# A two-layer decoder trunk on one core: plain fp32 products for three chunks of the first projection and half an out-projection, x loaded first, gate rows through DRAM, and a new order of steps

## The chip, the cores and the metric

One core of a Trainium2 chip. The metric is device time of one execution in microseconds (us), lower is better. The kernel before takes 633.34 us (median of 3 runs, 632.42 to 634.86).

## The reference

256 tokens of width 1024 go through two layers. Each layer has an attention sub-layer and an MLP; each of them is modulated by a conditioning vector c and closed by a LayerNorm:

```
mod = silu(c) @ ada_w + ada_b                    # per layer: shift1, scale1, gate1, shift2, scale2, gate2
h = x * (1 + scale1) + shift1
y = attention(h)                                 # h @ w_in -> q, k, v; rope; causal softmax; @ w_out
x = layer_norm(ALPHA * x + (1 + gate1) * y)      # layer 0: 16 heads of 64; layer 1: differential attention
h = x * (1 + scale2) + shift2
y = square(relu(h @ w_up)) @ w_down              # 1024 -> 4096 -> 1024
x = layer_norm(ALPHA * x + (1 + gate2) * y)
```

All data is float32. With one block of 256 keys, the block selection of layer 0 chooses nothing, and it is plain causal attention.

## The kernel before

The tokens are two blocks b of 128. Each dense product is made of 128x128 by 128x512 pieces, and keeps fp32 accuracy by **splitting**: both operands are written as hi + lo in the rounded type fp32r, and hi·hi, hi·lo and lo·hi are added in PSUM (`mm3`, `dense`, `dense2`: three matmuls for one product). A weight arrives by DMA in a raw tile (three buffers of 1 MB); `split_piece` makes hi with a cast on ACT (L499) and lo with a subtraction on DVE (L500), 1024 columns at a time, into eight buffers each. The activations are split in the same way.

The six vectors of `mod` are computed on DVE (`ada_rows`, L571 to L579): 128 rows of the transposed ada_w (512 KB, a tile aw) are multiplied by silu(c), spread over all partitions in sbc, and summed along the row. There are 96 such pieces. For the columns aw has two buffers; the first scale rows use the three buffers of bc.

**The first projection** is written out ahead of the table of steps. `first_operand(j)` takes chunk j of eight (128 of the 1024 input features): two pieces of ada, a slice of x, 768 KB of w_in (half of v, and q and k of head groups 0 and 1), a transposition of x on PE (L925), the modulation on ACT (L927), the split of both. `first_products(j)` adds 18 matmuls to six PSUM banks `kacc`. The other columns come later in `load_cols`: v group 1 (step v01), q and k of groups 2 and 3.

**The order** of everything else comes from the table `PROGRAM`: one word is one step. `aLVJ` is ada piece J of vector V in layer L, `V` and `Q` are projections (layer, block, group), `T` transposes q and k, `S` and `P` are scores and values of one (block, group), `o` and `O` load and multiply w_out, `G` spreads a gate vector over the partitions, `N` prepares the modulation after a LayerNorm, `C` is residual, LayerNorm and modulation of a block, `u`, `U`, `X`, `Y`, `d`, `D` are the MLP. `plan_issue` then simulates the engines with a table of costs and fixes each engine's queue: of what is ready it takes the instruction that stands first in the table. All loads go through SP's one queue, which issues in order and stands still while a load waits for its buffer.

The gate vector lies in columns (feature on partition). `step_gate` calls `bcast_cols`: eight PE transpositions of a column spread to 128x128 (L483) and two copies from PSUM on ACT (L485).

In layer 0 the attention has a score matmul of 64 rows for each head (L799), transposed probabilities (L780) and value matmuls (L873); these and layer 1's L839 are fp32 matmuls without a split, and each leaves two records in the trace. `split_oT` splits the attention's output, `out_proj` multiplies it. After the MLP of layer 1 comes a tail (`close_last`).

Of the kernel before, what the change touches and what calls it, by code (L numbers as in the profile page):

```python
# [21 lines left out]
P = 128  # L22
D = 1024
# [27 lines left out]
    u04 Y04 a051 a052 a116 a107 D002 a133 a140 d03 a120 u07 a130 Y06 a102 a142 a145 D011 d04 u05 D003 a144 a106
    D004 a105 Y05 a143 a146 D012 D013 D014 a057 Y07 a104 d05 D005 d06 D006 a115 D015 d07 D007 a111 G01 a114 a117
    N01 a135 C001 D016 D017 C011 v10 V100 q10 Q100 Q110 a136 a151 q11 V110 T100 Q111 T110 K01 S11 a123 Q101 a124
    R011 q12 T111 S10 a156 q13 Q103 Q113 T101 S12 P10 T103 a134 Q102 a132 S13 v11 o10 a125 Q112 a122 o11 u11 u10
    u14 a131 S16 F10 T102 P12 S14 F12 T112 V111 P11 d10 P13 a154 V101 P14 a155 F11 d11 P16 a126 a127 T113 u12
# [69 lines left out]
def _cost(i, e, psum_names):  # L125
# [4 lines left out]
    if e == 4:  # L130
# [3 lines left out]
        if "float32r" in str(aps[0].dtype):  # L134
            return (227 if n > 256 else 117 if n > 128 else 109), 170 + n * 0.43
# [42 lines left out]
class Planner:  # L178
# [3 lines left out]
    def __init__(self, ins, slots, psum_names, groups):  # L182
# [11 lines left out]
        for k, i in enumerate(ins):  # L194
# [9 lines left out]
            def hits(t, pm, fm, j, p2, f2):  # L204
                return p2 & pm and f2 & fm or t in psum_names and eng[j] != eng[k]
# [221 lines left out]
def tile_trunk(ctx: ExitStack, tc: tile.TileContext, x, c, moba_w_in, moba_w_out, diff_w_in, diff_w_out,  # L427
# [765 lines left out]
```

## Time and profile before

| | |
|---|---|
| median of 3 runs | 633.34 us |
| profiled execution | 632.71 us, of it 630.5 us between the first and the last instruction |
| PE, busy | 603.7 us (96%) |
| DVE, busy | 501.2 us (79%) |
| ACT, busy | 383.0 us (61%) |
| DMA | 158.25 MB, 251 GB/s over the span |

A PE record is longer than the time from one matmul's start to the next (a 128x512 matmul is shown with some 400 ns), so records overlap, a PE that is shown busy can still be slowed, and the pace of a run of matmuls is what counts. The other 2.2 us of the execution lie before the first and after the last instruction.

### The profile page before, as it was taken

What the parts mean: (1) busy time and instruction counts of PE and PEld (TensorE: products, weight loads), DVE (VectorE), ACT (ScalarE), POOL (GpSimd) and SP (SyncE); (2) the same over time, 40 slices, a digit from 0 to 9 for tenths busy, and PEclk for the clock granted to TensorE, in tenths of its full rate; (3) what the DMA queues carried; (4) which work ended last, traced back from release to release, by engine and by line L of the source; (5) the groups of instructions that cost most, each with busy time, mean ns of one, the idle gap of its engine ahead of it and who ended that gap; (6) DMA issues with size and microseconds to landing.
All of it is one profiled execution on the core that took longest, in us unless ns stands there. A gap on an engine that the chain in (4) does not pass through costs nothing.

```text
span 630.5 us, 8816 instructions
## 1 busy us (share of the span) xinstructions
PE 603.7 (96%) x3148; PEld 493.3 (78%) x3148; DVE 501.2 (79%) x899; ACT 383.0 (61%) x711; POOL 21.7 (3%) x36
## 2 busy tenths in 40 slices
PE   4999999989999999999999999999999999999995
PEld 3776776767788888888877878887788888888884
DVE  4899989899998887988799999868767556464557
ACT  3457788867745755565386566767657576363730
POOL 0000000011000000000011000111000000000001
PEclk9999999998999999999999999999999999999998
DMA  8999969878898987989777977333646664646201
GB/s 289 407 337 397 360 241 328 302 244 305 299 394 326 304 325 249 350 328 333 247 260 270 333 239 254 122 122 120 213 139 211 236 216 140 232 161 225 110 0 68
DMA packets 66086, 158.25 MB, mean 251 GB/s; under 512 B 4057, under 2 KB 21370, under 8 KB 66042
## 3 DMA queue, kind: packets, MB, share of 16 engines
q1 hardware_dynamic: 66042, 157.68, 70.3%
q8 instruction: 25, 0.41, 0.3%
q14 instruction: 19, 0.16, 0.1%
HBM read 156.62 MB, written 1.05 MB: 250 GB/s over the span
## 4 chain that ended last, share of the span: by engine, by line
PE 83%; DMA 7%; DVE 6%; issue 1%; POOL 1%; ACT 1%; SPq 1%; DVEq 0%; ACTq 0%; POOLq 0%
PE ac L553 18%; PE sc L553 12%; PE mm L1091 7%; PE tp L1091 7%; PE mm L536 7%; PE mm L538 7%; PE mm L537 7%; PE mm L1096 4%; PE tp L1096 4%; DMA raw<-in_moba_w_in_dram 3%; DMA aw<-in_ada_w_dram 2%; PE sc L799 2%; DVE lo L500 1%; PE tp L780 1%; PE tp L749 1%
## 5 line engine op out<-in xcount | busy, mean ns | idle before, releaser
L500 DVE TENSOR_TENSOR lo<-raw,hi 128x1024 fp32r<-128x1024 f32 x196 | 231.3, 1197 | 54.6 <-ACT hi L499 51.5
L499 ACT CAST hi<-raw 128x1024 fp32r<-128x1024 f32 x196 | 200.5, 1034 | 101.5 <-PE sc L553 41.0
L578 DVE CUSTOM_DVE_ANT_0 aw<-aw,sbc,tabT 128x1024 f32<-128x1024 f32 x96 | 121.6, 1278 | 8.9 <-DMA aw<-in_ada_w_dram 8.5
L536 PE MATMUL mm<-hi,hT 128*128 128x512 f32 x224 | 91.6, 410 | 6.8 <-ACT hT L676 3.3
L537 PE MATMUL mm<-lo,hT 128*128 128x512 f32 x224 | 89.5, 402 | 1.8 <-DVE lo L500 1.8
L538 PE MATMUL mm<-hi,hT 128*128 128x512 f32 x224 | 88.9, 399 | 0.3
L1091 PE MATMUL mm<-hT,hi 128*128 128x512 f32 x192 | 61.2, 396 | 0.0
L1091 PE MATMUL tp<-hT,hi 128*128 128x512 f32 x192 | 60.6, 395 | 0.0
L536 PEld LDWEIGHTS mm<-hi,hT 128*128 128x128 f32 x224 | 42.8, 191 | 17.2 <-ACT hT L676 4.2
L553 PE MATMUL ac<-lo,sTh 128*128 128x512 f32 x160 | 51.7, 397 | 0.0
L553 PE MATMUL ac<-hi,sTh 128*128 128x512 f32 x160 | 51.3, 396 | 0.0
L537 PEld LDWEIGHTS mm<-lo,hT 128*128 128x128 f32 x224 | 42.6, 190 | 11.2 <-DVE lo L500 3.0
L538 PEld LDWEIGHTS mm<-hi,hT 128*128 128x128 f32 x224 | 42.5, 190 | 10.7 <-DVE hT L677 2.1
L553 PE MATMUL ac<-hi,sTl 128*128 128x512 f32 x160 | 50.2, 392 | 0.0
L553 PE MATMUL sc<-lo,sTh 128*128 128x512 f32 x144 | 45.9, 394 | 0.0
L553 PE MATMUL sc<-hi,sTl 128*128 128x512 f32 x144 | 45.5, 393 | 0.0
L553 PE MATMUL sc<-hi,sTh 128*128 128x512 f32 x144 | 45.4, 393 | 0.0
L1096 PEld LDWEIGHTS tp<-hT,lo 128*128 128x128 f32 x192 | 34.7, 188 | 7.6
L1096 PEld LDWEIGHTS mm<-hT,lo 128*128 128x128 f32 x192 | 34.4, 188 | 7.1 <-DVE lo L500 0.2
L1096 PE MATMUL mm<-hT,lo 128*128 128x256 f32 x192 | 36.9, 279 | 0.0
L1096 PE MATMUL tp<-hT,lo 128*128 128x256 f32 x192 | 36.6, 279 | 0.0
L553 PEld LDWEIGHTS ac<-hi,sTh 128*128 128x128 f32 x160 | 29.5, 188 | 6.9 <-ACT hi L499 0.6
(173 smaller groups left out, 874.1 us busy)
## 6 DMA issues: line engine op xcount, KB each, us to landing
aw<-in_ada_w_dram SPq DMA_DIRECT2D x96, 512.0 KB, 5.4
raw<-in_mlp_w_up_dram SPq DMA_DIRECT2D x32, 1024.0 KB, 6.0
raw<-in_mlp_w_down_dram SPq DMA_DIRECT2D x32, 1024.0 KB, 7.0
raw<-in_diff_w_in_dram SPq DMA_DIRECT2D x16, 512.0 KB, 4.6
raw<-in_moba_w_in_dram SPq DMA_DIRECT2D x24, 256.0 KB, 6.9
raw<-in_moba_w_in_dram SPq DMA_DIRECT2D x8, 512.0 KB, 5.2
raw<-in_moba_w_out_dram SPq DMA_DIRECT2D x4, 1024.0 KB, 5.6
raw<-in_diff_w_in_dram SPq DMA_DIRECT2D x4, 1024.0 KB, 5.1
```

The lines of the kernel that those rows point to most:

```text
L499: act.copy(out=hi[:, :n], in_=raw_ap)
L500: vec.tensor_tensor(out=lo[:, :n], in0=raw_ap, in1=hi[:, :n], op=ALU.subtract)
L536: pe.matmul(dst, lhsT=xh, rhs=wh, start=start, stop=False)
L537: pe.matmul(dst, lhsT=xh, rhs=wl, start=False, stop=False)
L538: pe.matmul(dst, lhsT=xl, rhs=wh, start=False, stop=stop)
L553: pe.matmul(dsts[h], lhsT=a, rhs=w[:, h * 512:(h + 1) * 512], start=start and k == 0 and i == 0, stop=stop and k == n - 1 and i == 2)
L578: vec.tensor_tensor_reduce(out=aw, in0=aw, in1=sbc, scale=1.0, scalar=adab_cols(l, v)[:, j:j + 1], op0=ALU.mult, op1=ALU.add, accum_out=dst)
L749: pe.transpose(out=tp[:, i * P:(i + 1) * P], in_=nat[:, i * P:(i + 1) * P], identity=ident)
L780: pe.transpose(out=tp[:, s_ * P:(s_ + 1) * P], in_=mats[m][:, kb * P:(kb + 1) * P], identity=ident)
L799: pe.matmul(r[i, cpt][:, kb * P:(kb + 1) * P], lhsT=qk[l, b, g][rows, i, :], rhs=qk[l, kb, g][rows, 2 + i, :], start=True, stop=True)
L1091: pe.matmul(ps, lhsT=w[k][0][:, c_], rhs=x3[k], start=first, stop=last)
L1096: pe.matmul(ps[:, 0:S], lhsT=w[k][1][:, c_], rhs=x3[k][:, 0:S], start=False, stop=False)
```

## The change

- **Plain products in the first projection.** Chunks 0, 1 and 2 are not split: PE multiplies fp32 x by fp32 raw weights straight from the raw tile (24 matmuls in place of 72). Chunks 3 to 7 stay split. All 1024 columns of v are taken, so a chunk is 1 MB and eight products, and `kacc` takes all eight PSUM banks; step v01 with its 48 matmuls is gone from the later part.
- **x first.** Both blocks of x are loaded whole, the first ahead of all ada rows, transposed four chunks at a time, and kept in xT; the modulation then works in place.
- **Unread transposes.** 30 transpositions of sbc (`step_warm`) are put on PE among those of x. Nothing reads them.
- **Half the out-projection plain.** Feature half 1 of layer 0's w_out is loaded into hi and lo buffers as it is and multiplied in fp32 (`PLAINO` is (1,); 16 matmuls in place of 48); its oT isn't split.
- **Gate rows through DRAM.** A gate is one 128x8 transposition, a small copy on ACT, a write of 4 KB to DRAM and a broadcast load of 512 KB.
- **Two DVE operations of the rope become one**, and every second ada piece of layer 0's gate1, shift2 and scale2 uses bc's three buffers.
- **New order**: the first projection's steps are in the table now, and the whole table is another one (in the planner two numbers and one rule on PSUM change with it).

```diff
 PROGRAM = """
-    Q000 a020 V000 a046 v01 V010 Q001 a100 a043 V011 a024 a036 T000 S00 a032 Q010 a023 a045 q02 P00 a040 a025
+    W6 I1 A0 W5 I0 M0 B0 A1 M1 B1 m1 A2 B2 A3 A4 M4 A5 A6 W4 J0 B3 J1 B4 M2 A7 M7 m2 M6 B5 B6 M3 M5 J2 B7 a100
...
+    def plain_rows(w, r0):
+        ts = plain_tiles()
+        for k, t in enumerate(ts):
+            sp.dma_start(out=t, in_=w[r0 + k * P:r0 + (k + 1) * P, :])
+        return ts
...
-        ada_rows(l, v, j, cl[:, j:j + 1], "aw", 2)
+        tag = ("bc", 3) if l == 0 and v in (GATE1, SHIFT2, SCALE2) and j % 2 else ("aw", 2)
+        ada_rows(l, v, j, cl[:, j:j + 1], *tag)
...
+    PLAIN0 = (0, 1, 2,)
+    def step_warm(st, n):
+        ps = psum("ac")
+        for k in range(2 * n):
+            pe.transpose(out=ps[:, (k % 4) * P:(k % 4 + 1) * P], in_=sbc[:, (k % 8) * P:(k % 8 + 1) * P], identity=ident)
...
+        for s_ in (0, 2, 3, 1):
+            for b in range(2):
+                if j in PLAIN0:
+                    pe.matmul(kacc[b][(0, 3, 1, 2)[s_]], lhsT=xT[j // 4][:, j % 4, b * P:(b + 1) * P], rhs=ws[s_],
+                              start=j == 0, stop=j == KC - 1)
+                    continue
+                hi, lo = halves(hT0[j // 4], b)
+                mm3(kacc[b][(0, 3, 1, 2)[s_]], (hi[:, j % 4, :], lo[:, j % 4, :]), ws[s_], j == 0, j == KC - 1)
...
+        if l == 0 and g2 in PLAINO:
+            for k in range(4):
+                for h in range(2):
+                    pe.matmul(dsts[h], lhsT=oT[l, g2][:, k, b * P:(b + 1) * P], rhs=rows[k][:, h * 512:(h + 1) * 512],
+                              start=g2 == 0 and k == 0, stop=g2 == 1 and k == 3)
+            return
...
+    def step_gate_row(st, l, i):
+        row = st["row", l, i] = dram.tile([KC, P], F32, tag="row", name="row", bufs=1)
+        rs = small.tile([KC, P], F32, tag="grow", name="grow", bufs=1)
+        tp = psum("tp")
+        pe.transpose(out=tp[0:KC, 0:P], in_=cols[l, GATE1 if i == 0 else GATE2], identity=ident)
+        act.copy(out=rs, in_=tp[0:KC, 0:P])
+        sp.dma_start(out=row, in_=rs)
     def step_gate(st, l, i):
         g = st["gate", l, i] = ap_.tile([P, D], F32, tag="bc", name="gate", bufs=3)
-        bcast_cols(g, cols[l, GATE1 if i == 0 else GATE2])
+        row = st.pop(("row", l, i))
+        sp.dma_start(out=g, in_=row.rearrange("k p -> (k p)")[None, :].to_broadcast([P, D]))
```

Where the instructions stand. **PE, from its first instruction**, before (sbc and ccol: silu(c) and its columns; t: the table of biases; cs: the identity):

```order
L483 MATMUL tp<-cs,ccol 128x128 x8
L944 MATMUL tp<-cs,t_73 128x128
L925 MATMUL tp<-cs,x 128x128 x4
L536 MATMUL mm<-hi,hT 128x512
L536 MATMUL sc<-hi,hT 128x512
L536 MATMUL ac<-hi,hT 128x512
```

and now:

```order
L487 MATMUL tp<-cs,ccol 128x128 x8
L932 MATMUL tp<-cs,t_75 128x128
L954 MATMUL ac<-cs,sbc 128x128 x18
L942 MATMUL tp<-cs,x 128x128 x8
L954 MATMUL ac<-cs,sbc 128x128 x12
L942 MATMUL tp<-cs,x 128x128 x8
L995 MATMUL mm<-raw,xT 128x512 x2
L995 MATMUL sc<-raw,xT 128x512 x2
```

The unread transposes (L954) stand in PE's queue ahead of those of x, and all 16 transposes of x now stand ahead of the first product.

**DVE, from the mean and variance of the first LayerNorm (layer 0, block 0)**, before (col_530 and col_600 are scale2 and shift2; A and B, the modulation that ACT waits for; lo is the split of the MLP's weights):

```order
L652 BN_AGGR bna<-bns 128x2
L500 TENSOR_TENSOR lo<-raw,hi 128x1024
L578 ISA aw,col_530<-aw,sbc,tabT 128x1024
...
L594 TENSOR_TENSOR A_1411<-col_530,tabT 128x8
L595 TENSOR_TENSOR B_1412<-col_530,tabT_100 128x8
L500 TENSOR_TENSOR lo<-raw,hi 128x1024
L578 ISA aw,col_600<-aw,sbc,tabT 128x1024
L578 ISA col_600 128x1
L500 TENSOR_TENSOR lo<-raw,hi 128x1024
L596 TENSOR_TENSOR B_1412<-B_1412,col_600 128x8
```

and now (col_538 and col_555):

```order
L618 TENSOR_TENSOR A_1337<-col_538,tabT 128x8
L619 TENSOR_TENSOR B_1338<-col_538,tabT_102 128x8
L675 BN_STATS bns<-z 128x6
L503 TENSOR_TENSOR lo<-raw,hi 128x1024
L601 ISA aw,col_555<-aw,sbc,tabT 128x1024
L601 ISA col_555 128x1
L676 BN_AGGR bna<-bns 128x2
L620 TENSOR_TENSOR B_1338<-B_1338,col_555 128x8
```

A and B were finished after three ada pieces and four splits that stood behind the statistics; now B comes directly behind them, with the last ada piece ahead.

**SP, the loads around layer 0's first gate**, now (row and gate are the new write and broadcast load; the first LayerNorm needs gate, the modulation needs the three aw behind it):

```order
L600 DMA aw<-in_ada_w_dram 128x1024 x3
L1048 DMA row<-grow 8x128
L600 DMA aw<-in_ada_w_dram 128x1024 x2
L1053 DMA gate<-row 128x1024
L600 DMA aw<-in_ada_w_dram 128x1024 x3
L646 DMA bc<-in_ln_g_dram 128x1024
```

The gate's load stands two pieces of ada behind the write that it reads, and 41.8 MB of loads stand ahead of it in the queue, by the shapes; the last of the three aw ends at 43.4 MB. Before, the last ada piece of this LayerNorm ended at 43.9 MB.

## Rows read from the trace of the kernel before

**Rows 1.** The page's busy times by engine: us (share of the span), instructions.

```profile
PE 603.7 (96%) x3148; PEld 493.3 (78%) x3148; DVE 501.2 (79%) x899; ACT 383.0 (61%) x711; POOL 21.7 (3%) x36
```

**Rows 2.** Busy time of each engine between the LayerNorms (the cuts are the starts of BN_AGGR: layer 0 attention b0 130.8, b1 146.4, its MLP 318.5 and 331.5, layer 1 attention 430.7 and 447.9, its MLP 615.2). Columns: stretch, length, busy us and instructions of PE, PEld, DVE, ACT, POOL, then granted clock, DMA share, GB/s.

```profile
0.00:130.80 130.80, 116.43 (x659) 89.86 (x660) 112.88 (x267) 88.79 (x205) 0.29 (x5) 1.00 0.89 329
130.80:146.40 15.60, 12.37 (x52) 9.43 (x52) 15.14 (x29) 11.45 (x18) 2.54 (x2) 0.89 0.84 291
146.40:318.50 172.10, 172.10 (x861) 144.18 (x860) 149.21 (x202) 98.11 (x144) 2.56 (x2) 1.00 0.87 313
331.50:430.70 99.20, 99.00 (x555) 79.80 (x555) 88.02 (x232) 65.73 (x169) 9.36 (x18) 1.00 0.62 213
430.70:447.90 17.20, 16.64 (x76) 12.50 (x75) 15.98 (x22) 12.33 (x20) 1.25 (x3) 1.00 0.72 240
447.90:615.20 167.30, 167.16 (x840) 140.49 (x839) 96.32 (x115) 96.42 (x141) 0.81 (x2) 1.00 0.47 164
```

**Rows 3.** The same view with cuts at the start, the end of the first projection (52.4), the end of layer 0's out-projection (139.4), and the MLP's first products.

```profile
3.50:12.00 8.50, 3.33 (x13) 2.47 (x13) 3.43 (x8) 3.30 (x7) 0.00 (x0) 1.00 1.00 346
12.00:16.00 4.00, 3.97 (x9) 3.18 (x10) 3.99 (x5) 1.00 (x2) 0.00 (x0) 1.00 1.05 394
16.00:20.00 4.00, 4.00 (x21) 3.30 (x20) 3.73 (x8) 1.92 (x5) 0.00 (x0) 1.00 1.02 406
12.00:52.40 40.40, 37.73 (x156) 29.13 (x157) 37.46 (x78) 20.47 (x42) 0.00 (x0) 1.00 0.99 377
52.40:139.40 87.00, 83.81 (x532) 64.98 (x531) 79.59 (x195) 69.17 (x161) 2.54 (x2) 1.00 0.85 304
139.40:142.90 3.50, 0.44 (x3) 0.01 (x2) 3.50 (x7) 2.42 (x7) 0.00 (x0) 0.92 1.04 407
142.90:146.40 3.50, 3.50 (x10) 2.69 (x11) 3.50 (x7) 3.40 (x6) 0.00 (x0) 0.59 1.04 378
```

**Rows 4.** Undisturbed runs of one kind of matmul on the chain that ended last: start us, length us, engine, output, line, records.

```profile
124.30 1.05 PE mm L873 x16
357.28 1.09 PE sc L799 x16
428.12 0.97 PE mm L839 x8
514.89 0.87 PE tp L483 x8
600.63 10.89 PE ac L553 x48
```

**Rows 5.** The start, instructions in order of time: start us, length us, engine, line, operation, out<-in, shapes, count, and the idle time before with what ended it.

```profile
3.53 1.94 PE L483 MATMUL tp<-cs,ccol 128*128 128x128 f32 x8 [3.53 <-DMA cs<-in_constants_dram]
8.40 1.09 PE L925 MATMUL tp<-cs,x 128*128 128x128 f32 x4 [2.63 <-DMA x<-in_x_dram]
10.93 1.56 ACT L499 CAST hi<-raw 128x1024 fp32r<-128x1024 f32 x2 [0.53 <-DMA raw<-in_moba_w_in_dram]
12.03 0.80 PE L536 MATMUL mm<-hi,hT 128*128 128x512 f32 x1 [2.55 <-ACT hi L499]
```

**Rows 6.** PE's waits on the split and on the attention's chain, the same view.

```profile
25.86 0.50 PE L537 MATMUL mm<-lo,hT 128*128 128x512 f32 x1 [0.48 <-DVE lo L500]
39.25 0.44 PE L925 MATMUL tp<-cs,x 128*128 128x128 f32 x2 [1.26 <-ACT full L927]
55.42 0.50 PE L537 MATMUL mm<-lo,hT 128*128 128x512 f32 x1 [1.15 <-DVE lo L500]
110.46 0.66 PE L780 MATMUL tp<-cs,p 128*128 128x128 f32 x4 [0.53 <-ACT pT L782]
```

**Rows 7.** Groups of DVE and ACT instructions of the whole span: line, engine, operation, out<-in, shapes, count | busy us, mean ns of one | idle before, with its causes.

```profile
L500 DVE TENSOR_TENSOR lo<-raw,hi 128x1024 fp32r<-128x1024 f32 x188 | 226.3, 1219 | 54.6 <-ACT hi L499 51.5
L500 DVE TENSOR_TENSOR lo<-raw,hi 128x512 fp32r<-128x512 f32 x8 | 5.5, 682 | 0.0
L931 DVE TENSOR_TENSOR hT<-full,hT 128x128 fp32r<-128x128 f32 x16 | 3.9, 284 | 2.2 <-ACT hT L930 2.2
L892 DVE TENSOR_TENSOR sTl<-ac,sTh 128x256 fp32r<-128x256 f32 x4 | 1.7, 420 | 0.9 <-ACT sTh L891 0.9
L499 ACT CAST hi<-raw 128x1024 fp32r<-128x1024 f32 x188 | 196.2, 1052 | 101.5 <-PE sc L553 41.0 <-PE tp L1091 22.4 <-DMA raw<-in_moba_w_in_dram 14.0
```

**Rows 8.** Around the first LayerNorm of layer 0, instructions in order of time (SPq is SP's queue; the length of a load there is the time that it holds the queue).

```profile
124.56 9.05 SPq L577 DMA_DIRECT2D aw<-in_ada_w_dram  x3
139.15 1.22 DVE L500 TENSOR_TENSOR lo<-raw,hi 128x1024 fp32r<-128x1024 f32 x1
140.29 0.16 DVE L596 TENSOR_TENSOR B<-B,col 128x8 f32<-128x8 f32 x1
140.48 1.85 ACT L673 ACTIVATE full<-tp,B,A 128x128 f32<-128x128 f32 x5 [2.30 <-DVE B L596]
142.89 0.80 PE L536 MATMUL mm<-hi,hT 128*128 128x512 f32 x1 [3.06 <-ACT hT L676]
```

**Rows 9.** What SP's queue waited for, 60 to 150 us: us in total, times, longest.

```profile
SPq L577 <- DVE col L578: 21.2, 12, 3.2
```

**Rows 10.** Loads: out<-in, engine, operation, count, KB each, median us from issue to landing.

```profile
bc<-in_ln_g_dram SPq DMA_DIRECT2D x4, 512.0 KB, 7.3
ccol<-in_c_dram SPq DMA_DIRECT2D x1, 4.0 KB, 1.6
```

More of the change, by code (lines that the diff above doesn't have):

```diff
@@ L51 @@
[L51 to L55, printed above, removed]
@@ L402, in run @@
         return r
-    store = type(s_.bass_ap.tensor).__name__ == "Tile"
+    t = s_.bass_ap.tensor
+    store = type(t).__name__ == "Tile" and str(t.space) != "DRAM"
     on, off = (s_, o) if store else (o, s_)
@@ L885, in split_oT @@
         key = l, g // 2
+        if l == 0 and g // 2 in PLAINO:
+            if key not in oT:
+                oT[key] = ap_.tile([P, 4, 2 * P], F32, tag="sTh", name="oT", bufs=2)
+            act.copy(out=oT[key][:, (g % 2) * 2:(g % 2) * 2 + 2, b * P:(b + 1) * P],
+                     in_=tp[:, 0:256].rearrange("p (k t) -> p k t", t=P))
+            return
         if key not in oT:
@@ L967, in tile_trunk @@
-    vec.reduce_sum(out=ldot, in_=lprod, axis=AX.X)
-    act.activation(out=ldot, in_=ldot, func=AF.Exp)
-    vec.tensor_tensor(out=ldot[:, 0:1], in0=ldot[:, 1:2], in1=ldot[:, 0:1], op=ALU.subtract)
-    vec.tensor_scalar(out=ldot[:, 0:1], in0=ldot[:, 0:1], scalar1=-LAMBDA_INIT, scalar2=None, op0=ALU.add)
-    nlam = small.tile([P, 1], F32, name="nlam")
-    tps = psum("tp")
-    pe.matmul(tps[:, 0:1], lhsT=ones[0:1, :], rhs=ldot[:, 0:1], start=True, stop=True)
-    vec.tensor_copy(out=nlam, in_=tps[:, 0:1])
+    xT = [ap_.tile([P, 4, 2 * P], F32, tag="sTl", name="xT", bufs=2) for _ in range(2)]
@@ new lines, in step_first_weights @@
+    def step_first_weights(st, j):
+        raw = raw_tile()
+        wr = moba_w_in[0][j * P:(j + 1) * P, :]
+        sp.dma_start(out=raw[:, 0:1024], in_=wr[:, 2 * D:3 * D])
+        for s_ in range(2):
+            sp.dma_start(out=raw[:, 1024:2048].rearrange("p (g s n) -> p s g n", g=2, s=2)[:, s_],
+                         in_=wr[:, s_ * D:s_ * D + 512].rearrange("p (g n) -> p g n", n=256))
+        if j in PLAIN0:
+            st["w0", j] = [raw[:, i * 512:(i + 1) * 512] for i in range(4)]
+            return
+        st["w0", j] = [(h_[:, c_:c_ + 512], l_[:, c_:c_ + 512])
+                       for h_, l_ in (split_piece(raw[:, 0:1024]), split_piece(raw[:, 1024:2048])) for c_ in (0, 512)]
@@ L1030, in step_v @@
     def step_v(st, l, b, g2):
-        if l == 0 and g2 == 0:
-            ps = kacc[b][0]
+        if l == 0:
+            ps = kacc[b][3 * g2]
         else:
@@ L1042, in step_qk @@
             w = st["wq", l, g]
-            ps = unit(w, block_ops(st["x", 2 * l], b))
+            if l == 0 and g in PLAIN:
+                ps = psum("mm")
+                for k in range(KC):
+                    pe.matmul(ps, lhsT=xT[k // 4][:, k % 4, b * P:(b + 1) * P], rhs=w[k], start=k == 0, stop=k == KC - 1)
+            else:
+                ps = unit(w, block_ops(st["x", 2 * l], b))
         rope_qk(l, b, g, ps)
```

173 lines of the change are left out of this document (99 added, 74 removed).

## The prediction

> **What bounds the kernel now.** I read the busy times first, then the busy time between the LayerNorms, then the pace of undisturbed matmuls, and last PE's waits in the stretches where it lost time. The page says PE is busy 96% of the span [rows 1]: only less work on PE, or less waiting in the few places that still wait, can shorten it. In the two MLPs PE is busy all the time (172.1 of 172.1 us, 167.2 of 167.3) [rows 2]; there nothing is to be won but PE work. Layer 0's attention is another matter: to the second LayerNorm at 146.4 us DVE is busy 112.9 + 15.1 = 128.0 us [rows 2], 91% of the time since it began at about 6 us, and DMA's share is 0.89 over the first 130.8 us. Three engines are close to their limits there, and they stop each other.
>
> How much PE loses there follows from paces. A 128x512 fp32r matmul takes 10.89 / 48 = 0.227 us, a transposition 0.87 / 8 = 0.109, and 16 records of layer 0's scores or values take 1.09 and 1.05 us [rows 4]. The first projection is 144 matmuls and 12 transposes of x between 12.0 and 52.4 us (156 records) [rows 3]: 32.7 + 1.3 = 34.0 us of work in 40.4. From there to the end of the out-projection at 139.4 stand 48 matmuls for v group 1, 96 for q and k, 96 for the out-projection (54.5 us), 96 transposes (10.5), and 96 records each of scores and values (12.8): 77.8 us of work in 87.0. So PE loses 6.4 + 9.2 = 15.6 us between 12.0 and 139.4. Behind that it stands 3.5 us until the MLP's first product, which waits for B, late on DVE [rows 8], and then the granted clock is 0.59 for 3.5 us [rows 3]: eight products at the lower level, 1.2 GHz, some 0.2 us longer each, 1.6 us. Compared with a PE that never stopped, the MLP begins at 139.4 + 3.5 + 1.6 = 144.5.
>
> **The change, part by part.**
>
> *Plain products.* 40 fp32 matmuls take the place of 120. The trace has no plain 512-column product, but it has full fp32 products of 128 columns: 8 records, four products, in 0.97 us, the last record's end included [rows 4]. By columns that is at most 0.97 us for 512 columns; four passes at the price of the fp32r matmul are 0.91. A group of eight ends with a tail that a row of products doesn't show, so I take 0.89 and keep 0.85 to 0.97. Each costs 0.89 - 0.68 = 0.21 us more on PE than the three that it replaces, 8.4 us in all. What goes is off PE: up to the second LayerNorm DVE loses eight splits of 512 columns (8 x 0.682 = 5.5), four net of 1024 (4.9), four of oT (1.7) and two or so of hT and the rope [rows 7], 14.3 us together, so 113.7 us are left. ACT loses about as much, which ends nothing, since it waits itself.
>
> *The start.* Ahead of the first weights 2.2 MB are loaded in both orders; they were there at 10.9 us [rows 5], x now with them. Four transposes, a copy and a modulation on ACT then take about 1.6 us, the first half of the weights comes 0.52 MB later (1.5 us at 346 GB/s [rows 3]), and no split follows. First product at 13.0 instead of 12.03. All transposes of x are then done. In the four us from 12.0 PE got through 9 matmuls, in the next four 21 [rows 3]: the pace of 1.2 GHz, although the row prints a clock of 1.00. That cost 2.0 us. The 30 unread transposes fill the time from 5.5 us; I take it that after them the first products run at the full pace.
>
> *What the sum takes for the attention.* Work on PE from the first product: 24 x 0.89 + 120 x 0.227 = 48.6 us for the first projection with all of v, then 96 x 0.227 = 21.8, out-projection 48 x 0.227 + 16 x 0.89 = 25.1, 89 transposes 9.7, scores and values 12.8: 118.0 us. That ends at 131.0 plus the waits. Of the 15.6 us of waits now, 2.0 are the low clock, 4.4 the split and ada in the first projection and 1.2 lo of v group 1 [rows 6]; the plain chunks and the empty v01 step take most of these away. About 8 are the attention's chains between PE, DVE and ACT. DVE's share falls from 91% to 113.7 of about 137 us, 83%, and q and k products of two groups now stand between the attention's pieces. I keep 7 us of waits; the bounds are 1 and the 15.6 of now. The MLP then begins at 138.0 without the gap: B stands directly behind the statistics, and PE has out-projection work of block 1 (12.6 us) while block 0 is normalized. Gain 144.5 - 138.0 = **6.5 us**.
>
> *DMA.* The last ada piece that this LayerNorm needs ends at 43.4 MB in SP's queue; at 377 GB/s [rows 3] that is 118 us, ahead of the 130 or so at which it is wanted. What held the queue were ada buffers (SP waited 21.2 us for DVE's col in 60 to 150 us [rows 9], 9.05 us for one group of three [rows 8]); there are five of them now for these vectors. Cost 0, with this cover of some 10 us.
>
> *Gates.* Seven PE transposes fewer each. The one in the attention is counted above; the other three give 21 x 0.109 = **2.3 us** in stretches where PE is always busy. The load is queued tens of products ahead in the MLPs, so the way through DRAM costs nothing there.
>
> *Layer 1.* Same work, another order; DVE keeps its 104 us of 116 between 331.5 and 447.9 [rows 2]. 0, with 4 us to either side.
>
> *Sum.* 630.5 - 6.5 - 2.3 = 621.7 us of span; with the 2.2 us around it, **624 us**. The profiled execution (632.71) is 0.6 below the median of the runs, which doesn't move the forecast. A measurement of this kernel can tell about 0.5%, 3.2 us, from no change: 630.2 to 636.5 counts as the same.
>
> **The rivals.**
>
> *The clock stays low at the start.* Thirteen transposes ran before 12.03 us and the first products still went at 0.43 us [rows 3, 5]; but PE had been idle for 2.55 us before them, so the trace leaves it open. If transposes don't raise the clock, those in the queue take 0.217 each (1.94 us for eight with the tail [rows 5]), the second x comes through 2.5 us later and the first 4 us lose 2.0 again: 624 + 4.5 = 628.5. The Trainium skill (TensorE: Matmul & The Clock Gate, Part 4: PE-mode transpose) says just this, that transposes don't count as busy for the clock. By that rule the unread transposes are a loss, and the sum is 628.5. Chance 0.18.
>
> *The waits stay.* Each of the three engines has less to do or the same, but chains of latency decide, not shares: 15.6 us of waits instead of 7 give 632.6. For it: PE waited for ACT and DVE in pieces of half a us [rows 6], which a freer DVE need not shorten. Against it: the new order puts more independent products between them. Chance 0.17.
>
> *The waits all but vanish*, and layer 1 gains too: 1.5 us instead of 7, and 4 us from layer 1, 614.5. Chance 0.12.
>
> *The gate comes late.* The gate no longer costs 1.5 us on PE and ACT but a write that must land (1.6 us for a small transfer), a wait of SP's queue for it and a load of 512 KB (7.3 us for such a broadcast) [rows 10]: 7.4 us more on LayerNorm's chain. At the same time a raw buffer of a plain chunk is freed only after its products (7.1 us for 2.1 MB, 295 GB/s instead of 377), which over three chunks costs DMA 4.7 us. If the loads are what block 0's LayerNorm waits for, the MLP begins 12.1 us later and the kernel takes 630.5 + 12.1 - 2.3 + 2.2 = 642.5, slower. It decides from the point where the gate's load is issued less than about 10 us before block 0's out-projection ends. Against it: 10 us of cover by the DMA sum above. Chance 0.08.
>
> **How the numbers follow.** The forecast (618 to 630) has 0.45, the rivals 0.18, 0.17, 0.12 and 0.08. Faster: nearly all of the forecast, the last but one, two thirds of the low clock and a little of the case of the waits, 0.72. Same: most of the case of the waits and the rest of the low clock, 0.18. Slower: the late gate and a bad order of layer 1 on top of the waits, 0.10. The range 614.5 to 636 leaves out the late gate and half of the best case; the bounds of the plain product (40 x 0.04 below, 40 x 0.08 above) lie inside.
>
> **What would show it.** Plain products at about 0.45 us a record and two records each; the first at 13 us and at that pace at once (right) or at 0.86 (low clock); 48 to 50 us of first projection with waits under 3 us; the MLP's first product about 138 us with no gap and a granted clock of 1.00 ahead of it; DVE near 114 us to the second LayerNorm; two short records of SP around the gate. The prediction is wrong if the plain product costs over 1 us, if PE waits for gate or B in layer 0, or if layer 1's attention takes over 120 us.

## The result: 624.4 us, 1.4% less time

The changed kernel takes 624.4 us (median of 4 runs, 623.45 to 624.98); the kernel before took 633.20 beside it (median of 4). The ratio is 0.9856, with an interval of 0.9833 to 0.9880. The profiled execution has a span of 622.4 us, 8.1 less than before. The forecast was 624.0.

The page's busy times, to be held against [rows 1]: PE works 1.6 us more in a span that is 8.1 us shorter, DVE and ACT some 13 to 17 us less.

```profile
PE 605.3 (97%) x3110; PEld 485.4 (78%) x3110; DVE 484.6 (78%) x857; ACT 370.3 (59%) x689; POOL 27.2 (4%) x36
```

The changed kernel's busy time between the LayerNorms, columns as in [rows 2]:

```profile
0.00:129.10 129.10, 123.67 (x662) 89.04 (x663) 104.76 (x243) 82.67 (x190) 0.29 (x5) 1.00 0.96 353
129.10:141.50 12.40, 11.25 (x42) 6.74 (x40) 11.43 (x20) 6.97 (x14) 2.60 (x2) 1.00 0.64 214
141.50:311.60 170.10, 169.59 (x845) 142.01 (x844) 143.88 (x196) 96.79 (x143) 2.48 (x2) 1.00 0.86 309
324.40:426.70 102.30, 101.03 (x563) 81.03 (x562) 91.70 (x232) 68.92 (x172) 11.87 (x18) 1.00 0.65 222
426.70:439.50 12.80, 12.16 (x58) 9.58 (x57) 11.32 (x18) 9.73 (x17) 2.49 (x2) 1.00 0.63 205
439.50:607.10 167.60, 167.45 (x835) 139.86 (x834) 97.96 (x116) 94.97 (x139) 2.49 (x2) 1.00 0.52 176
```

In the first stretch DMA's share rose from 0.89 to 0.96. The granted clock, 0.89 between layer 0's two LayerNorms before, is 1.00. In layer 1 the attention became longer and the stretch between its LayerNorms shorter, 115.1 us together after 116.4; its MLP is as long as before (167.6 and 167.3).

PE from 5 to 18 us, in order of time (start, length, count, and the idle time before with what ended it):

```profile
5.38 3.79 PE L954 MATMUL ac<-cs,sbc 128*128 128x128 f32 x18
9.00 1.04 PE L942 MATMUL tp<-cs,x 128*128 128x128 f32 x8
9.88 1.47 PE L954 MATMUL ac<-cs,sbc 128*128 128x128 f32 x12
12.21 1.06 PE L942 MATMUL tp<-cs,x 128*128 128x128 f32 x8 [0.86 <-DMA x<-in_x_dram]
14.49 1.98 PE L995 MATMUL mm<-raw,xT 128*128 128x512 f32 x4 [1.22 <-ACT xT L978]
16.31 1.88 PE L995 MATMUL sc<-raw,xT 128*128 128x512 f32 x4
```

Eighteen unread transposes take 3.79 us, the eight of x behind them 1.04. The granted clock is printed as 1.00 for this whole stretch, so the pace has to tell: up to about 8.8 us the transposes start 0.213 us apart, behind it 0.109, which is the step from the lower level (1.2 GHz) to the higher (2.4 GHz), behind nothing but transposes. The second half of x came late, and the first plain product starts at 14.49. From its second record on the plain products run at 0.429 us per record, two records each: 0.859 us.

PE's stretches up to the MLP (columns as in [rows 2]; at 135.50 the last record of the out-projection begins, at 137.25 the MLP's first product):

```profile
14.49:60.00 45.51, 45.51 (x158) 29.62 (x159) 36.71 (x61) 20.02 (x30) 0.00 (x0) 1.00 1.04 401
60.00:135.50 75.50, 75.50 (x471) 54.25 (x470) 69.98 (x184) 59.17 (x154) 2.60 (x2) 1.00 0.92 329
135.50:137.25 1.75, 0.60 (x2) 0.00 (x0) 1.75 (x3) 1.75 (x6) 0.00 (x0) 1.00 0.88 334
```

The DMA engines are at least as busy as they were in the first projection before (0.99) [rows 3], but PE is now busy for all of it. Between its first product and the MLP's PE now idles 1.15 us; before it was 2.67 to 52.4 us, 3.19 to 139.4 and 3.06 ahead of the MLP [rows 3], 8.9 in all.

PE and DVE at the first LayerNorm of layer 0, to be held against [rows 8]: B (L620) comes directly behind the mean and variance, and PE's gap is 1.15 us in place of 3.06. It is no longer a wait for B, which is done at 129.41, but for the transposes of z (L693) and what ACT makes of them.

```profile
129.13 0.20 DVE L676 BATCH_NORM_AGGREGATE bna<-bns 128x2 f32<-128x12 f32 x1
129.25 0.16 DVE L620 TENSOR_TENSOR B<-B,col 128x8 f32<-128x8 f32 x1
132.14 0.55 DVE L681 TENSOR_SCALAR z<-z,bna,rs 128x512 f32<-128x512 f32 x1 [0.46 <-POOL rs L651]
132.61 0.15 DVE L683 SCALAR_TENSOR_TENSOR nm<-bna,rs 128x1 f32<-128x1 f32 x1
134.20 1.04 PE L693 MATMUL tp<-cs,z 128*128 128x128 f32 x8
135.08 1.02 PE L1033 MATMUL sc<-plain,oT 128*128 128x512 f32 x2
137.25 0.50 PE L559 MATMUL mm<-hi,hT 128*128 128x512 f32 x1 [1.15 <-ACT hT L700]
```

What SP's queue waited for from 60 to 150 us (us in total, times, longest): the gate's load waited 1.4 us for the write of its rows to land. Ada's buffers still hold the queue, 22.8 us where it was 21.2 [rows 9].

```profile
SPq L600 <- DVE col L601: 22.8, 14, 3.3
SPq L1053 <- DMA row<-grow: 1.4, 1, 1.4
```

**Where the 8.1 us are.** The first product starts 2.5 us later (14.49 where it was 12.03). From it to the MLP's first product it takes 122.8 us instead of 130.9: 8.1 less. From there to the end it takes 485.15 instead of 487.6: 2.5 less, of which 1.6 is the low clock behind the old gap (an estimate from [rows 3]).

### The profile page after: what moved, and what is told of

Its sections match the earlier page's. It is cut to its first block, busy times and chain, and to the rows that moved or that the text cites. A ratio compares the mean times of both kernels' runs of the same rounds, so it can differ in the third digit from the quotient of the medians.

```text
span 622.4 us, 8672 instructions
## 1 busy us (share of the span) xinstructions
PE 605.3 (97%) x3110; PEld 485.4 (78%) x3110; DVE 484.6 (78%) x857; ACT 370.3 (59%) x689; POOL 27.2 (4%) x36
## 4 chain that ended last, share of the span: by engine, by line
PE 79%; DVE 11%; DMA 3%; issue 2%; POOL 2%; ACT 1%; SPq 0%; DVEq 0%; POOLq 0%; ACTq 0%
PE ac L576 16%; PE sc L576 10%; PE tp L1167 6%; PE mm L561 6%; PE mm L1167 6%; PE mm L560 6%; PE mm L559 6%; PE tp L1172 3%; PE mm L1172 3%; DVE lo L503 3%; DVE aw L601 2%; DMA aw<-in_ada_w_dram 2%; PE sc L823 2%; DMA x<-in_x_dram 1%; PE tp L804 1%
## 5 line engine op out<-in xcount | busy, mean ns | idle before, releaser
L503 DVE TENSOR_TENSOR lo<-raw,hi 128x1024 fp32r<-128x1024 f32 x182 | 218.1, 1218 | 59.1 <-ACT hi L502 57.6
L502 ACT CAST hi<-raw 128x1024 fp32r<-128x1024 f32 x182 | 189.3, 1053 | 90.8 <-PE sc L576 23.4
L559 PE MATMUL mm<-hi,hT 128*128 128x512 f32 x202 | 81.0, 402 | 1.2 <-ACT hT L700 1.2
L560 PE MATMUL mm<-lo,hT 128*128 128x512 f32 x202 | 80.3, 397 | 0.0
L561 PE MATMUL mm<-hi,hT 128*128 128x512 f32 x202 | 79.9, 397 | 0.0
L576 PE MATMUL ac<-hi,sTh 128*128 128x512 f32 x152 | 48.0, 395 | 0.0
L559 PEld LDWEIGHTS mm<-hi,hT 128*128 128x128 f32 x202 | 38.0, 188 | 9.3 <-ACT hT L700 2.0
L561 PEld LDWEIGHTS mm<-hi,hT 128*128 128x128 f32 x202 | 37.9, 188 | 8.3 <-DVE hT L701 0.4
L560 PEld LDWEIGHTS mm<-lo,hT 128*128 128x128 f32 x202 | 38.0, 188 | 7.5 <-issue 0.4
L576 PE MATMUL sc<-lo,sTh 128*128 128x512 f32 x136 | 42.8, 392 | 0.0
L576 PE MATMUL sc<-hi,sTl 128*128 128x512 f32 x136 | 42.5, 391 | 0.0
L576 PEld LDWEIGHTS ac<-hi,sTl 128*128 128x128 f32 x152 | 28.4, 188 | 5.8
```

Source lines behind the costliest of these rows:

```text
L502: act.copy(out=hi[:, :n], in_=raw_ap)
L503: vec.tensor_tensor(out=lo[:, :n], in0=raw_ap, in1=hi[:, :n], op=ALU.subtract)
L559: pe.matmul(dst, lhsT=xh, rhs=wh, start=start, stop=False)
L560: pe.matmul(dst, lhsT=xh, rhs=wl, start=False, stop=False)
L561: pe.matmul(dst, lhsT=xl, rhs=wh, start=False, stop=stop)
L576: pe.matmul(dsts[h], lhsT=a, rhs=w[:, h * 512:(h + 1) * 512], start=start and k == 0 and i == 0, stop=stop and k == n - 1 and i == 2)
```

## The experiments

Three marks of each kernel's trace carry the comparison: first product, MLP's first product, and the rest (span less that mark). Ratios are to the kernel before, run on the same chip beside each; its median there lay between 633.2 and 634.6 us, so a difference of two medians below is uncertain by that much. The marks are those of one profiled execution. For no_warm (629.9 us), split_out (640.1) and gate_pe (631.2) that was the slowest of its executions, for all_undone (637.0) and b_plainout (639.7) the fastest. How far the marks scatter shows in no_warm, unread_out and unread_first, which keep the changed kernel's order: their rest lies between 3.1 us above and 1.0 below its 485.2.

| kernel | median us | ratio (interval) | first product | MLP's first | rest |
|---|---|---|---|---|---|
| before | 633.2 | 1 | 12.03 | 142.89 | 487.6 |
| the change | 624.4 | 0.9856 (0.9833 to 0.9880) | 14.49 | 137.25 | 485.2 |
| no_warm | 626.9 | 0.9884 (0.9859 to 0.9908) | 13.99 | 139.58 | 488.2 |
| split_first | 638.0 | 1.0073 (1.0046 to 1.0101) | 14.68 | 142.24 | 493.6 |
| split_out | 636.8 | 1.0031 (1.0013 to 1.0049) | 13.79 | 143.56 | 494.3 |
| gate_pe | 630.5 | 0.9929 (0.9906 to 0.9952) | 13.85 | 138.53 | 490.5 |
| all_undone | 637.8 | 1.0059 (1.0035 to 1.0083) | 14.94 | 145.91 | 488.9 |
| b_plainfirst | 635.4 | 1.0012 (0.9996 to 1.0029) | 9.86 | 143.61 | 489.5 |
| b_plainout | 642.4 | 1.0126 (1.0081 to 1.0170) | 11.88 | 149.42 | 488.1 |
| before_warm | 633.1 | 0.9991 (0.9968 to 1.0014) | 11.90 | 142.79 | 487.8 |
| order_117 | 625.2 | 0.9871 (0.9839 to 0.9902) | 13.73 | 136.78 | 485.9 |
| unread_out | 627.1 | 0.9890 (0.9870 to 0.9909) | 13.77 | 139.22 | 484.8 |
| unread_first | 626.2 | 0.9876 (0.9861 to 0.9891) | 13.39 | 139.92 | 484.2 |
| plain_four | 623.3 | 0.9829 (0.9813 to 0.9846) | 13.52 | 137.27 | 484.1 |

### One part of the change undone

**no_warm**: the unread transposes are left out.

```diff
-    W6 I1 A0 W5 I0 M0 B0 A1 M1 B1 m1 ...
+    I1 A0 I0 M0 B0 A1 M1 B1 m1 ...
```

> The changed kernel without the 30 unread transposes; every other queue keeps its order. If transposes raise PE's clock, as the changed kernel's trace suggests (the first 18 at 0.21 us each, from 9.0 us on 0.11), then the 16 transposes of x run at 0.21 again, the first product comes about 0.5 to 1 us later than 14.5 us, and the first 4 us of plain products run at 0.86 us a record instead of 0.43, which costs 2.0 us: 626.5 to 627.5 us. If the clock rises for another reason, pace and start stay as they are: 624.4 us. If the unread transposes hold up those of x, the first product comes earlier and the time is 623 us.

PE of this kernel, in order of time:

```profile
6.15 1.97 PE L942 MATMUL tp<-cs,x 128*128 128x128 f32 x8 [0.38 <-ACT sbc L489]
10.88 1.94 PE L942 MATMUL tp<-cs,x 128*128 128x128 f32 x8 [2.76 <-DMA x<-in_x_dram]
13.99 3.78 PE L995 MATMUL mm<-raw,xT 128*128 128x512 f32 x4 [1.17 <-ACT xT L978]
```

All transposes of x run at the low clock, and the first six records stand 0.853 us apart instead of 0.429; the pace changes at 19.8 us. From the first product to the MLP's it takes 125.6 us instead of 122.8, nearly all of it these six records (2.5 us). In the trace the unread transposes are worth what they do to the clock at the start. By the ratios it is 1.8 us, by the medians 2.5, and the two intervals overlap. The rest of this execution is 3.1 us longer in the same order: behind the MLP of layer 0 PE stood 1.93 us for the LayerNorm, and the granted clock was 0.65 from 319 to 323 us.

**split_first**: chunks 0 to 2 split like the others, with all of v (the three words m0 to m2 leave the table with it).

```diff
-    PLAIN0 = (0, 1, 2,)
+    PLAIN0 = ()
```

> The changed kernel with chunks 0 to 2 of the first projection split like the others (no plain products there). PE has 24 x 0.18 = 4.3 us less work, DVE 7.3 and ACT 6.3 us more in the first 50 us. My theory (the plain products take away waits on the split): the first product comes 1 to 2 us later, PE waits 4 to 6 us more between 14 and 60 us, 625 to 628 us. Rival (the plain products cost on PE what they save in waits, the gain is the order's): 620 to 624 us.

Its window from 14.5 to 60 us, columns as in [rows 2], and then PE and ACT around PE's longest wait:

```profile
14.50:60.00 45.50, 37.18 (x145) 29.72 (x146) 42.48 (x66) 24.66 (x33) 0.00 (x0) 0.89 1.05 406
```

```profile
39.61 1.04 ACT L502 CAST hi<-raw 128x1024 fp32r<-128x1024 f32 x1 [1.74 <-DMA raw<-in_moba_w_in_dram]
42.20 1.04 ACT L502 CAST hi<-raw 128x1024 fp32r<-128x1024 f32 x1 [1.55 <-DMA raw<-in_moba_w_in_dram]
44.98 1.22 PE L561 MATMUL mm<-hi,hT 128*128 128x512 f32 x2 [5.72 <-DVE hT L986]
```

With 1.05 and 406 GB/s the loads run as fast as in the changed kernel, PE is busy 37.2 us where that kernel has 45.5, and ACT waits for the weights' DMA. PE's longest wait ends with DVE's hT, and DVE is busy 42.5 of the 45.5 us; but the chain that ended last in this stretch consists of loads for 74% of its length (ada rows 40.5%, weights 33.9%), where in the changed kernel it is PE's matmuls alone. So with all chunks split the loads set the pace, and a plain product is work that PE does on bytes that are already there. Its price on PE (0.859 instead of 0.681 us) is paid in time in which PE would wait. A part of the loss is the clock again: it fell behind a wait of 2.46 us at the start and is 0.50 from 15.6 to 19.0 us. The rest is 8.4 us longer too. There the plan is another one (some 230 of DVE's 857 instructions stand elsewhere in its queue), and what share of that the splits themselves make isn't shown.

**split_out**: both halves of the out-projection split.

```diff
-    PLAIN, PLAINO = (), (1,)
+    PLAIN, PLAINO = (), ()
```

> The changed kernel with the whole out-projection of layer 0 split. PE has 16 x 0.18 = 2.8 us less work, DVE 4 splits of 1024 and 4 of oT more (6.5 us) ahead of the second LayerNorm. My theory (DVE's share decides the waits there): the waits rise by more than the 2.8 us, 625 to 627 us. Rival (PE's work decides): 621.5 to 622.5 us.

DVE and PE at layer 0's first LayerNorm, and PE's windows from there:

```profile
127.82 1.28 DVE L662 TENSOR_TENSOR z<-ac,gate 128x512 f32<-128x512 f32 x2
136.38 0.20 DVE L676 BATCH_NORM_AGGREGATE bna<-bns 128x2 f32<-128x12 f32 x1
139.33 0.55 DVE L681 TENSOR_SCALAR z<-z,bna,rs 128x512 f32<-128x512 f32 x1 [0.45 <-POOL rs L651]
139.87 0.15 DVE L683 SCALAR_TENSOR_TENSOR nm<-bna,rs 128x1 f32<-128x1 f32 x1
140.02 2.08 PE L693 MATMUL tp<-cs,z 128*128 128x128 f32 x8 [5.29 <-DVE nm L683]
```

```profile
134.00:140.00 6.00, 0.73 (x4) 0.28 (x3) 5.55 (x13) 0.00 (x0) 2.54 (x2) 0.95 0.65 179
140.00:143.50 3.50, 2.08 (x8) 1.42 (x8) 3.49 (x5) 3.17 (x8) 0.00 (x0) 0.50 0.96 370
143.50:146.50 3.00, 2.94 (x7) 2.36 (x8) 2.95 (x5) 3.00 (x7) 0.00 (x0) 0.50 0.88 290
146.50:149.50 3.00, 3.00 (x8) 2.32 (x8) 3.00 (x5) 0.46 (x1) 0.83 (x1) 0.50 0.24 87
```

PE stood 5.29 us because the LayerNorm began late on DVE: its first step (z, L662) runs at 127.82 instead of 118.8, the mean and variance come at 136.38 instead of 129.13. From there to nm, for which PE waits, both kernels take 3.5 us, and both wait there for POOL (0.45 and 0.46 us). Ahead of z the chain that ended last goes over the write of the gate's row, for which SP's queue stood 2.2 us (0.8 in the changed kernel), the load of an ada piece issued behind it (117.71, 5.60 us), and the ada pieces on DVE. Then the clock is at the lower level for some ten us more, and PE does 15 matmuls in 6 us that it would do in 3.4. The clock is low at 331 to 337 us too, behind the next LayerNorm, and from 13.1 us on, so that the first seven records were slow (3.0 us). A gap costs its length and then the clock. How much of the loss the splits' work alone makes, unread_out tells below.

**gate_pe**: the gate by PE transpositions and copies again (the words g00 to g11 leave the table with it).

```diff
-        row = st.pop(("row", l, i))
-        sp.dma_start(out=g, in_=row.rearrange(...)[None, :].to_broadcast([P, D]))
+        bcast_cols(g, cols[l, GATE1 if i == 0 else GATE2])
```

> The changed kernel with the gates spread by eight PE transposes and two ACT copies, as before; no write to DRAM. My theory (PE work in stretches where PE never stops is time): 4 x 7 x 0.109 = 3.1 us longer, 627.5 us. Rival (the two MLPs did not get shorter in the changed kernel, so the saving was lost to other waits): 624 to 625 us.

6.1 us slower than the change by the medians, 4.6 by the ratios; in the profiled execution 1.3 at the MLP's first product and 5.3 in the rest. In front of the MLP PE idles 1.69 us instead of 1.15, and from 139.0 to 142.4 the granted clock is 0.51 where it was 1.00. The planner moves other work too (some 100 of DVE's 857 instructions stand elsewhere in its queue), so that the loss can't be read as the price of 28 transposes (28 x 0.109 = 3.1 us).

**all_undone**: the four edits above together; left of the change are the order, x first, the merged v, five ada buffers and the rope.

```diff
-    W6 I1 A0 W5 I0 M0 B0 A1 M1 B1 m1 ...
+    I1 A0 I0 M0 B0 A1 M1 B1 ...
...
-    PLAIN0 = (0, 1, 2,)
+    PLAIN0 = ()
...
+        bcast_cols(g, cols[l, GATE1 if i == 0 else GATE2])
...
-    PLAIN, PLAINO = (), (1,)
+    PLAIN, PLAINO = (), ()
```

> The changed kernel with every part undone that can be undone alone: no unread transposes, all chunks and the whole out-projection split, gates on PE. What stays is the new table, x first, all of v in the first projection, five ada buffers and the shorter rope. Theory 1 (the new table and the plain products were fitted to each other; the table alone gives nothing): as slow as the first two undone or slower, 634 to 642 us. Theory 2 (most of the gain is the order's): 626 to 630 us.

Slower than the kernel before by 0.6%. What is left of the change is of no use by itself. Taken singly the four parts seem worth 2.5 to 13.6 us by the medians and add up to 34.6, together they are worth 13.4: the losses of single undoings overlap and hold a good deal that isn't the part. The table is the changed kernel's, with the words of the missing parts taken out. A table made anew for this kernel, or for the kernel before, was not run, so what a better order alone could give stays open.

### One part alone on the kernel before

**b_plainfirst**: chunks 0 to 2 plain, with the columns that they had.

```diff
+        if j < 3:
+            return full, [raw[:, i * 512:(i + 1) * 512] for i in range(3)]
...
+                    pe.matmul(kacc[b][s_], lhsT=ws[0][:, b * P:(b + 1) * P], rhs=ws[1][s_], start=j == 0, stop=False)
```

> The kernel before with chunks 0 to 2 of its first projection plain, nothing else changed (18 plain matmuls in place of 54). PE has 3.2 us more work, the first product needs no split. If waits on the split cost time in the first 52 us, PE's waits there (6.4 us) fall by 4 or more and the gain is 1 to 3 us: 630 to 632. If DMA bounds that stretch (its share is 0.99), nothing moves: 632.5 to 634.

No difference that can be told (0.9996 to 1.0029). The first product starts 2.2 us earlier, since it waits for no split, and yet the first projection ends when it did: its last record starts at 52.51 us, before 52.54. The dearer products (18 x 0.178 = 3.2 us) are paid out of waits, and nothing is won: DMA's share from 12.0 to 52.4 us is 0.99 in both kernels, and the last chunks come with their loads. The MLP's first product is 0.7 us later.

**b_plainout**: half the out-projection plain.

```diff
+        if (l, g2) == (0, 1):
+                    pe.matmul(dsts[h], lhsT=oT[l, g2][:, k, b * P:(b + 1) * P], rhs=rows[k][:, h * 512:(h + 1) * 512],
+                              start=False, stop=k == 3)
```

> The kernel before with half of layer 0's out-projection plain, nothing else changed. PE has 2.8 us more work, DVE 6.5 us less ahead of the second LayerNorm. In the changed kernel undoing this part cost some 11 us, as PE then stood 7 us at the first LayerNorm. If the part has that worth by itself, the 3.5 us gap before the MLP goes and the time is 627 to 630; if the worth lay in a table fitted to it, it is 632 to 636.

Slower by 1.3%. PE and DVE ahead of the MLP:

```profile
141.44 2.74 PE L991 MATMUL sc<-plain,oT 128*128 128x512 f32 x6
149.42 0.79 PE L536 MATMUL mm<-hi,hT 128*128 128x512 f32 x1 [5.24 <-ACT hT L676]
145.01 1.27 DVE L578 CUSTOM_DVE_ANT_0 aw<-aw,sbc,tabT 128x1024 f32<-128x1024 f32 x1
146.81 0.15 DVE L596 TENSOR_TENSOR B<-B,col 128x8 f32<-128x8 f32 x1
```

In this order B is finished at 146.96, behind its ada piece, although DVE has less to do. The gap grows from 3.06 to 5.24 us, and the products are dearer by 16 x 0.178 = 2.8 us. Less work on DVE is worth nothing where the order leaves the late piece late.

**before_warm**: 30 unread transposes ahead of x's.

```diff
+    for n in (12, 10, 8):
+        ps = psum("ac")
+        for k in range(n):
+            pe.transpose(out=ps[:, (k % 4) * P:(k % 4 + 1) * P], in_=sbc[:, (k % 8) * P:(k % 8 + 1) * P], identity=ident)
```

> The kernel before with 30 unread transposes of sbc ahead of the first transposes of x, nothing else changed. If transposes raise the clock, the first products (12 to 16 us) go at 0.23 us instead of 0.43 and PE is 2 us ahead there; the time falls by that only if DMA doesn't bound the stretch to 52 us: 631 us. If DMA bounds it, the pace changes and the time doesn't: 632.5 to 634. If they don't raise it, neither changes.

No difference (0.9968 to 1.0014). PE at the start:

```profile
5.34 4.01 PE L949 MATMUL ac<-cs,sbc 128*128 128x128 f32 x30
9.19 0.60 PE L925 MATMUL tp<-cs,x 128*128 128x128 f32 x4
11.90 0.50 PE L536 MATMUL mm<-hi,hT 128*128 128x512 f32 x1 [2.11 <-ACT hi L499]
13.56 0.63 PE L537 MATMUL mm<-lo,hT 128*128 128x512 f32 x1
16.12 0.63 PE L537 MATMUL mm<-lo,hT 128*128 128x512 f32 x1
```

The transposes do raise the clock here as well (x's four take 0.60 us, before 1.09 [rows 5]), and the first six matmuls go at full pace. Then seven go at 0.427 us: the clock, up since 6.5 us, fell once more behind an idle time of 2.11 us (granted 0.50 from 13.4 to 16.6 us). Here the unread transposes bring nothing; in the changed kernel x's own transposes follow them so closely that PE stands less.

### The order, and the work on DVE and ACT

**order_117**: one number of the planner.

```diff
-            return (227 if n > 256 else 115 if n > 128 else 109), 170 + n * 0.43
+            return (227 if n > 256 else 117 if n > 128 else 109), 170 + n * 0.43
```

> Only a number of the planner's table changes (an fp32r matmul of 256 columns is taken as 117 ns, not 115), so the same work is issued in another order; nothing else differs. Theory one, the table of steps is fitted so closely that any other plan loses: 627 to 632 us, with new waits of PE somewhere in the attention of a layer, and then part of what the kernels with one part undone lost is misfit and not the part's worth. Theory two, the order is robust and those losses are the parts' own: 623.5 to 625.5 us, the MLP's first product still at 137 to 138 us.

625.2 us, not to be told from the change, and the MLP's first product at 136.78: theory two by time and mark. But the number moved little: some 40 of PE's 3110 instructions and 27 of DVE's 857 stand elsewhere in their queues, where split_out moved some 140 of DVE's and split_first some 230. So a small change of order costs nothing; that a large one does so isn't shown, and the losses of the undone kernels can still be the order's.

**unread_out** (order kept): the plain tiles of the out-projection are split as well, and nothing reads the halves.

```diff
+    def split_unread(raw_ap, loads):
...
+        act.copy(out=hi, in_=raw_ap)
...
+        vec.tensor_tensor(out=lo, in0=raw_ap, in1=hi, op=ALU.subtract)
...
             sp.dma_start(out=t, in_=w[r0 + k * P:r0 + (k + 1) * P, :])
+            split_unread(t, [nc.cur_bb.bb.instructions[-1].name])
```

> The order of the changed kernel is kept as it is on every engine; in it stand four more casts on ACT (4.2 us) and four more subtractions on DVE (4.9 us) of the plain tiles of the out-projection, right behind their loads. Nothing reads them. Theory one, the relief of DVE and ACT ahead of the first LayerNorm is what the plain out-projection is worth: 628 to 630 us, the MLP's first product at 141 to 142 us. Theory two, it isn't the work but the order that the kernel without it lost by: 624 to 625.5 us, the MLP's first product within 1 us of 137.3.

627.1 us; the MLP's first product is 2.0 us later, the rest 0.4 shorter. It falls between the theories. From 100 to 130 us DVE is busy 29.24 us (28.45 in the change) and PE 29.07 (30.00). So the relief of DVE and ACT from the weights' splits is worth about 2 us (1.6 by the spans, 2.2 by the ratios); the intervals overlap. split_out had 6.3 us at the MLP and 9.2 in the rest; what goes beyond the 2 us is order and clock, and in part an execution that was the slowest of its twelve.

**unread_first** (order kept): the same for the raw weights of chunks 0 to 2.

```diff
         if j in PLAIN0:
+            loads = [i.name for i in nc.cur_bb.bb.instructions[-3:]]
+            for q in range(2):
+                split_unread(raw[:, q * 1024:(q + 1) * 1024], loads)
```

> The order is kept as it is; six more casts on ACT (6.3 us) and six more subtractions on DVE (7.3 us) of the raw weights of chunks 0 to 2 stand in it right behind their loads, and nothing reads them. DVE, 36.7 us busy of the 45.5 from the first product to 60 us, would come to 44. Theory one, DVE's work is what the split chunks lost: the ada rows come late, PE waits 3 to 7 us before 60 us, 627 to 631 us. Theory two, the loads set the pace of the first projection and the plain products only fill PE's time: waits before 60 us stay under 1 us, 624 to 625.5 us.

626.2 us, the MLP's first product 2.7 us later although the first product is 1.1 earlier; the rest is 1.0 shorter. DVE and PE at the first split chunk:

```profile
34.06 1.22 DVE L513 TENSOR_TENSOR spare<-raw,spare 128x1024 f32<-128x1024 f32 x1
35.19 1.22 DVE L503 TENSOR_TENSOR lo<-raw,hi 128x1024 fp32r<-128x1024 f32 x1
36.46 0.50 PE L571 MATMUL mm<-lo,hT 128*128 128x512 f32 x1 [1.34 <-DVE lo L503]
```

Here an unread subtraction stands ahead of one that PE waits for. Theory two falls: in this kernel the loads alone do not set the pace, DVE's 7.3 us cost PE 2.9 in waits (1.34, 1.24 and 0.35). Theory one has the mechanism, with waits and time a little below its ranges (3 to 7 us, 627 to 631). By the ratios the whole is 1.3 us, and the intervals overlap.

**plain_four**: chunk 3 plain as well.

```diff
-    PLAIN0 = (0, 1, 2,)
+    PLAIN0 = (0, 1, 2, 3,)
```

> Chunk 3 is plain as well: eight plain products of 0.859 us in place of 24 matmuls of 0.227, 1.42 us more on PE in a stretch in which PE has no waits; DVE and ACT lose two more splits. Theory one, PE paces the first projection as it stands: 625.8 us, every product behind it 1.4 us later. Theory two, the loads pace it and PE has room: 624.4 us, no later than now. A plan that fits worse would show as waits of PE outside the first projection, 627 us and more.

623.3 us, the shortest of all; its interval overlaps that of the change. The first projection, from its first record to its last, takes 1.39 us more (13.52 to 62.68 where it was 14.49 to 62.26), as the sum had it (1.42), so PE paces this stretch and theory one has the mechanism. The price is given back by a first product that came 0.97 us earlier, by the gap ahead of the MLP (0.29 instead of 1.15 us) and by a rest 1.0 shorter, which unread_first has too, without a fourth plain chunk; so theory two has the time, and by chance in part. Whether a fourth plain chunk gains anything stays open.

## Why the prediction was right

It held to 0.4 us, and its main step held, the wait that goes in layer 0's attention: PE's idle time there fell from 8.9 to 1.15 us. That the total came so near is luck: several terms were off and made up for each other. Up to the MLP's first product the kernel is 0.75 us ahead of the sum, behind it 1.5 us slower than the sum (485.15 for 483.7).

- **Plain product.** 0.859 us measured, 0.89 taken, bounds 0.85 to 0.97. Over 40 products that is 1.2 us less.
- **The start.** 13.0 taken, 14.49 measured in this execution, 13.4 to 14.0 in the seven other kernels that begin with plain products and x first: the second half of x landed at 12.07 us and not with the weights at 10.9. The sum was short by 0.4 to 1.5 us. b_plainfirst, which loads x in slices, has its first product at 9.86.
- **The clock at the start.** The first products ran at full pace, as taken. The rival by which the clock stays low did not come; before_warm and split_out show that it can come even with unread transposes, behind idle time, and no_warm shows that the price of slow first products is near what the rival had (2.5 us of records against 2.0). The Trainium skill (TensorE: Matmul & The Clock Gate, Part 4: PE-mode transpose) says that transposes don't count as busy for the clock. The trace disagrees: behind transposes alone the pace of transposes went from 0.213 to 0.109 us at 8.8 us.
- **Waits.** 125.0 us were taken from the first product to the MLP's, 122.8 came. With the product's true price that is 116.8 us of work and 6.0 of waits, where I kept 7 without a gap. Of these 6.0 only 1.15 are idle time of PE, all of it the gap ahead of the MLP; the others stand in no gap, but in paces a little longer than those of undisturbed runs. That gap did not go, it shrank from 3.06 us, with no low clock behind it. The MLP began at 137.25, forecast 138.0.
- **Why they went.** The forecast named DVE's share. The runs show two things beside it. In the first projection the loads run as fast in split_first as in the changed kernel (406 and 401 GB/s), and plain products with all of v turn PE's waiting there into work. DVE's and ACT's lighter load is worth 2.0 us in the out-projection and 2.7 in the first projection, by the MLP's first product of the two kernels with the order kept (1.6 and 1.7 by their spans). And B directly behind the statistics is the order's doing: with plain products on the old order (b_plainout) the gap grew. None of the three parts that were run alone gains anything, and neither does what all_undone leaves; x first, the gate rows and the shorter rope were not run alone. How the gain divides, and what a table made anew without plain products would give, stays open.
- **DVE.** 113.7 us to the second LayerNorm taken, 116.2 measured (104.76 + 11.43). The operations that went are those that the sum took: the lengths of DVE's records in this stretch fall by 14.2 us. But records of neighbours overlap (a split is shown with 1.22 us and the next instruction starts 1.13 us later), and the busy time, which counts an overlap once, fell by 11.8.
- **DMA and the gate in layer 0.** Cost 0, as taken. DVE first uses the gate at 118.8 us and does not wait for it, but its load was issued at 113.27, 5.5 us ahead: less cover than the 10 us that I had worked out, and within the condition under which the rival of the late gate was to decide. It did not.
- **Gates elsewhere.** This term did not show. Behind the MLP's first product 2.3 us were to be gained beyond the low clock; 0.9 came. Layer 0's MLP took 174.35 us from its first product to its LayerNorm, before 175.6 less 1.6 for the clock, 174.0: the seven transposes fewer bought nothing there. Of what took their place the trace shows a wait of 0.3 us for lo; the rest isn't shown. gate_pe does not give the term back either, since its order differs. This is the term of the sum that failed.
- **Layer 1.** 0 taken, 1.3 us gained in its attention, inside the 4 us allowed. This gain stands in the place of the one that the gates were to bring.

## What to carry over

Where loads set the pace, a dearer form of the matmul that needs no preparation is free up to the time in which PE would wait (b_plainfirst: 3.2 us more work, the same end), and behind that point it costs its price (plain_four: 1.39 us for 1.42): measure PE's busy time in that stretch with both forms before counting matmuls. To find the worth of a part in a planned order, keep the order and add the removed work back unread; undoing the part moves the order, and the loss then holds gaps and low clock elsewhere. Look at where a late LayerNorm begins, and not only at the steps just ahead of PE's gap: in split_out its first step already came nine us late. Have the small inputs of a LayerNorm, as B here, done ahead of long independent work, since a gap of PE is paid twice where the clock falls.

## What the runs showed of the hardware

- A 128x512 fp32 matmul without a split takes 0.859 us at the full clock and 1.706 at the low one, as two equal records; an fp32r one takes 0.227 at the full clock.
- Transposes alone raised TensorE's clock in each kernel with unread ones, but not at a fixed point: PE began at 3.3 to 3.6 us each time, and the pace changed between 6.3 us (split_out) and 9.3 (order_117). What sets the point is open. The granted clock is printed as 1.00 on both sides of the change there; only the pace tells.
- A clock that had risen fell again behind short idle times at the start (1.40 and 1.22 us in split_out, 2.11 in before_warm, 2.46 in split_first), while 0.86 and 1.22 us in the changed kernel left it up. Ahead of the MLP, 1.15 us left it up in the changed kernel, and behind 1.69 us in gate_pe it was 0.51.
- A write of 4 KB to DRAM held the load that reads it back on SP's queue by 1.4 us.
